# Tracing each convolution of a hybrid SSD/attention block one tile ahead of its user, on one Trainium2 core

## The chip, the cores and the metric

The kernel runs on one core of a Trainium2 chip. The metric is the device time of one execution in microseconds (us). A core has a matrix engine (PE, with its weight loads shown apart as PEld), a vector engine (DVE), a scalar engine for activations (ACT), a general engine (POOL) and a sync engine (SP) whose queue issues most DMAs. Every engine runs its own instructions strictly in the order of its list, and the engines wait for one another through semaphores.

## The reference, cut to what matters

Two layers, each a token mixer followed by a mixture of experts. Layer 0 mixes with a bidirectional Mamba-2 scan (SSD), layer 1 with attention. The change touches the SSD mixer alone:

```python
def project(u):
    z, xbc, dtr = jnp.split(u @ in_w, [D_INNER, D_INNER + CONV_DIM], axis=-1)
    xbc = jax.nn.silu(dwconv_centred(xbc, conv_w, conv_b))          # width 5, per channel
    xs, Bm, Cm = jnp.split(xbc, [...], axis=-1)                     # 2048, 8*128, 8*128 channels
    dt = jax.nn.softplus(dtr... + dt_bias)
def ssd_chunked(xs, dt, A, Bm, Cm, h0):                             # chunks of 128 tokens
    seg = exp(where(tri, acum[..., :, None] - acum[..., None, :], -inf))
    cb = einsum('bclgn,bcsgn->bcgls', Cc, Bc)                       # the product B C, per group
    y_diag = einsum('bcgrls,bcsgrp->bclgrp', cb[:, :, :, None] * seg, xdt)
    states = einsum('bcsgn,bcgrs,bcsgrp->bcgrpn', Bc, decay_end, xdt)
    h = dec * h + st                                                # scan over the chunks
    y_off = einsum('bclgn,bcgrpn,bcgrl->bclgrp', Cc, h_prev, exp(acum))
    return y_diag + y_off
y = y_forward + flip(y_backward) + D_skip * xs
out = rmsnorm(y * silu(z), norm_w) @ out_w
```

There are 1280 tokens (256 context, 1024 latent), that is 10 chunks of 128, 8 groups of B and C with 4 heads of 64 channels each.

## The kernel before, in words

Channels are cut into tiles of 128: 16 tiles of x, 8 of B, 8 of C, 16 of the gate z. **A tile of the convolution** (`conv_tile`) fetches its weights by DMA (L309), splits them into a high part on ACT (L311) and a low part on POOL (L314, twice), and projects the tokens on PE in three blocks of 256, 512 and 512: 72 matmuls at L54 to L56, 24 of them with 256 columns and 48 with 512. ACT copies each block out (L344, L345), DVE adds the other four taps (L349, four times), ACT takes a tangent (L353) and DVE applies it (L354, twice).

**A group** is one tile of B, one of C, the transpose of B (`Btm`), the product B C (`cb`, L513) and then two **cores**, one for each x tile of the group. `core` transposes its x tile (L363), runs the backward states (L396, L382) and then five pairs of chunks. For each pair it needs a decay matrix `Eb`: a DMA on SP's queue spreads a row over the partitions (L405), POOL masks two halves (L408, twice), ACT takes eight exponentials (L413), POOL adds the halves (L416), DVE multiplies by `cb` (L417). There are three `Eb` buffers, so the DMA of pair 4 can start only when pair 1's last output matmul (L463) is done, pair 5's after pair 2's, and the next core's first after pair 3's. The state that enters a chunk goes through PE (L442), DVE (L451) and POOL (`yos`, L452) before PE adds it to the output (L460 with `Eb`, L463 with `yos`). DVE adds the skip term (L467) and SP stores the tile (L469).

**Order.** The lists of the engines are made by a list scheduler: what is traced earlier has priority, and a step takes its place when its inputs and a buffer are free by the scheduler's estimates. A tile's buffers come from pools with a fixed count: one of B (`h_lo`), two each of C, x, raw and of the weights, three PSUM banks for projections (`in_ps`), one for transposes (`tr_ps`, used by L363 and L513), two for outputs (`y_ps`). The gates of the first two z tiles (`gate`, with `halves` giving its two scratch tiles) follow the last core and fill PE beside it; the gates from the third on use other pools.

Of the kernel before, what the change touches and what calls it, by code (L numbers as in the profile page):

```python
# [9 lines left out]
F32 = mybir.dt.float32  # L10
# [8 lines left out]
P = 128  # L19
# [10 lines left out]
NG = 8  # L30
# [10 lines left out]
class Net:  # L41
# [128 lines left out]
    def ssd(self):  # L170
# [53 lines left out]
        gp = tc.alloc_tile_pool(name="grp", bufs=1)  # L224
# [81 lines left out]
        def weights(c0):  # L306

            raw = wp.tile([P, KT, P], F32, name="w_raw")
            nc.sync.dma_start(raw, wv[:, :, c0:c0 + P])  # L309
            w = [wp.tile([P, KT, P], F32R, name=f"w{k}") for k in range(2)]  # L310
            nc.scalar.activation(w[0], raw, AF.Copy)  # L311
            for k in range(0, KT, 4):
                sl = slice(k, k + 4)
                nc.gpsimd.tensor_tensor(w[1][:, sl], raw[:, sl], w[0][:, sl].bitcast(F32), op=OP.subtract)  # L314
            return w

        def proj(w, b, pin=pin):
            t0, n = BLK[b]
            ps = pin.tile([P, 512], F32, name="in_ps")
            for k in range(KT):  # L320
                self.mm3(ps[:, :n], [w[m][:, k] for m in range(2)], [hT(m, k, b) for m in range(2)],
                         k == 0, k == KT - 1)
            return ps[:, :n], t0, n

        PAD = {0: 2, 1: 262, 2: 774}
        PTOK = TOK + 4

        def at(c, n=1):

            o = c * P + (4 if c >= NCT else 0)  # L330
            return slice(o, o + n * P)

        def conv_tile(ci, dst):

            w = weights(DI + ci * P)
            next(mods, None)
            raw = gp.tile([P, 1288], F32, name="raw", bufs=2)
            nc.gpsimd.memset(dst[:, 256:260], 0.0)
            nc.gpsimd.memset(raw[:, 0:2], 0.0)
            nc.gpsimd.memset(raw[:, 258:262], 0.0)  # L340
            nc.gpsimd.memset(raw[:, 1286:1288], 0.0)
            for b in range(3):
                ps, t0, n = proj(w, b)
                nc.scalar.activation(raw[:, PAD[b]:PAD[b] + n], ps, AF.Copy)  # L344
                nc.scalar.activation(dst[:, PAD[b] - 2:PAD[b] - 2 + n], ps, AF.Identity,  # L345
                                     bias=self.pcol[:, 160 + ci:161 + ci], scale=self.pcol[:, 64 + ci:65 + ci])

            for w_ in (0, 1, 3, 4):
                nc.vector.scalar_tensor_tensor(dst, raw[:, w_:w_ + PTOK], self.pcol[:, 32 * w_ + ci:32 * w_ + ci + 1],  # L349
                                               dst, op0=OP.mult, op1=OP.add)  # L350
            for t0, n in ((0, 642), (642, 642)):
                th = raw[:, t0:t0 + n]
                nc.scalar.activation(th, dst[:, t0:t0 + n], AF.Tanh)  # L353
                nc.vector.scalar_tensor_tensor(dst[:, t0:t0 + n], th, 1.0, dst[:, t0:t0 + n], op0=OP.add, op1=OP.mult)  # L354

        def transposed(src, name, pool):

            o = pool.tile([P, NT, P], F32, name=name)
            for c0 in range(0, NT, 4):
                n = min(4, NT - c0)  # L360
                ps = ptp.tile([P, 4, P], F32, name="tr_ps")
                for q in range(n):
                    nc.tensor.transpose(ps[:, q], src[:, at(c0 + q)], self.ident)  # L363
                nc.scalar.activation(o[:, c0:c0 + n], ps[:, :n], AF.Copy)
            return o
# [132 lines left out]
                    nc.scalar.activation(th[:, :n], yd[:, :n], AF.Square)  # L498
                    nc.gpsimd.tensor_tensor(acc[:, t0:t0 + n], first[:, t0:t0 + n], th[:, :n], op=OP.add)

        for g in range(NG):
            BT = hp.tile([P, PTOK], F32, name="BT", tag="h_lo")
            CT = gp.tile([P, PTOK], F32, name="CT", bufs=2)
            conv_tile(16 + g, BT)
            conv_tile(24 + g, CT)
            Btm = transposed(BT, "Btm", gp)
            cb = gp.tile([P, NT, P], F32, name="cb")
            for c0 in range(0, NT, 4):
                n = min(4, NT - c0)
                ps = ptp.tile([P, 4, P], F32, name="tr_ps")  # L510
                for q in range(n):
                    sl = at(c0 + q)
                    nc.tensor.matmul(ps[:, q], BT[:, sl], CT[:, sl], start=True, stop=True)  # L513
                nc.scalar.activation(cb[:, c0:c0 + n], ps[:, :n], AF.Copy)
            for h in range(2):
                xT = gp.tile([P, PTOK], F32, name="xT", bufs=2)
                conv_tile(2 * g + h, xT)
                core(2 * g + h, xT, CT, Btm, cb)
        for _ in mods:
            pass  # L520

# [1 line left out]
        zt = adp.tile([P, 4, 512], F32, name="adw")  # L523
        acc0 = hp.tile([P, TOK], F32, name="acc0", tag="h_lo")
        turns = 0

        def halves():
            nonlocal turns
            turns ^= 2
            return zt[:, turns], zt[:, turns + 1]  # L530
        for ct in range(early):
            gate(ct, weights(ct * P), pin, halves, acc0, acc0 if ct else None)
        for p_ in (pst, ptp, pin, co, gp, adp, cs):
# [983 lines left out]
```

## Time and profile before

| | |
|---|---|
| median of 3 runs | 3840.92 us (3840.58 to 3845.42) |
| the profiled execution's own time | 3852.41 us |
| its span in the trace | 3850.6 us |
| mean granted PE clock over the span | 0.973 |
| PE busy | 3562.8 us, 93% of the span |
| the SSD stage that the change touches | about 130 to 990 us of the span |

Busy time is the time in which an engine worked; what stands in brackets behind an instruction of the trace is the idle time of the engine just before it and what ended it. The granted clock is a share of full speed.

### The profile page before, as it was taken

The numbers are of one execution on the slowest core, as the hardware profiler recorded it, in microseconds if no ns is written. First come the engines' busy times: TensorE is split into PE (matmuls) and PEld (weight loads), VectorE is DVE, ScalarE is ACT, GpSimd is POOL, SyncE is SP. The second block draws the span as 40 slices with busy tenths as digits, with TensorE's granted clock in tenths as the row PEclk, the third lists the DMA queues.
The fourth block names the chain that finished last, engine by engine and source line by source line (L and its number), as shares of the span: only waits on it lengthen the run. The fifth ranks groups of instructions, "written<-read, shape, count | busy, mean of one in ns | idle before, by whom it ended". The sixth has DMA issues, their size and how long they took to land.

```text
span 3850.6 us, 56599 instructions
## 1 busy us (share of the span) xinstructions
PE 3562.8 (93%) x21156; PEld 2674.7 (69%) x21156; DVE 2594.0 (67%) x3675; ACT 2024.8 (53%) x3310; POOL 1811.8 (47%) x1356
## 2 busy tenths in 40 slices
PE   6999999999898998999999998899999976999997
PEld 3776777777787775666666767667777655777765
DVE  4776777777533376666666665555666587999988
ACT  4544444445323234555555545477777534777665
POOL 2345554455443334566666662221111115777786
PEclk8999999999999998999999998999999987999999
DMA  5333422222544336888888872100000346999994
GB/s 191 108 104 116 128 90 83 79 77 90 161 137 142 119 117 244 315 305 311 319 320 304 287 238 91 39 17 1 1 1 12 118 168 265 371 382 379 343 339 163
DMA packets 296803, 681.10 MB, mean 177 GB/s; under 512 B 22568, under 2 KB 148400, under 8 KB 290384
## 3 DMA queue, kind: packets, MB, share of 16 engines
q1 hardware_dynamic: 271824, 615.50, 44.6%
q0 software_dynamic: 12752, 39.33, 4.2%
q10 hardware_dynamic: 11952, 22.65, 1.8%
q8 instruction: 167, 2.74, 0.3%
q14 instruction: 108, 0.88, 0.1%
HBM read 611.97 MB, written 62.82 MB: 175 GB/s over the span
## 4 chain that ended last, share of the span: by engine, by line
PE 37%; DVE 11%; issue 6%; DMA 5%; POOL 4%; ACT 2%; SPq 0%; ACTq 0%; POOLq 0%; DVEq 0%
DVE m_w L728 6%; PE pv L1177 5%; PE S L1143 4%; PE a_tr L1164 4%; PE acc L54 4%; PE acc L56 4%; PE acc L55 4%; POOL m_w L725 3%; PE cacc L695 3%; DMA m_raw<-in_moe_w_dram 3%; PE o_ps L55 1%; PE o_ps L56 1%; PE o_ps L54 1%; PE qkv L56 1%; PE qkv L54 1%
## 5 line engine op out<-in xcount | busy, mean ns | idle before, releaser
L728 DVE TENSOR_TENSOR m_w<-m_raw,m_w 128x1792 fp32r<-128x1792 f32 (+1 forms) x384 | 890.5, 2342 | 251.8 <-ACT m_w L722 249.5
L722 ACT ACTIVATE m_w<-m_raw 128x2048 fp32r<-128x2048 f32 x384 | 732.6, 1916 | 485.9 <-DMA m_raw<-in_moe_w_dram 268.1
L725 POOL TENSOR_TENSOR m_w<-m_raw,m_w 128x256 fp32r<-128x256 f32 (+1 forms) x384 | 824.7, 2175 | 346.1 <-ACT m_w L722 343.5
L54 PE MATMUL in_ps<-hh,w 128*128 128x512 f32 (+1 forms) x1152 | 423.6, 368 | 7.7 <-DVE th L491 7.7
L55 PE MATMUL acc<-m_w,xl 128*128 128x512 f32 x1024 | 407.9, 399 | 22.3 <-DVE m_w L728 13.7
L56 PE MATMUL in_ps<-hh,w 128*128 128x512 f32 (+1 forms) x1152 | 420.7, 365 | 0.0
L55 PE MATMUL in_ps<-hl,w 128*128 128x512 f32 (+1 forms) x1152 | 418.7, 363 | 0.0
L54 PE MATMUL acc<-m_w,xl 128*128 128x512 f32 x1024 | 407.2, 404 | 4.5 <-ACT xl L48 4.5
L56 PE MATMUL acc<-m_w,xl 128*128 128x512 f32 x1024 | 402.1, 393 | 0.0
L413 ACT ACTIVATE Eb<-Eb,ebias 128x128 f32<-128x128 f32 x640 | 199.4, 391 | 165.2 <-POOL Eb L408 163.5
L1147 DVE TENSOR_REDUCE mx<-S 128x1 f32<-128x1024 f32 x128 | 155.7, 1216 | 181.2 <-PE S L1143 179.2
L1194 POOL TENSOR_TENSOR q<-s 64x128 f32<-64x128 f32 x128 | 58.7, 459 | 415.2 <-DVE mx L1152 347.4
L55 PEld LDWEIGHTS acc<-m_w,xl 128*128 128x128 f32 x1024 | 193.9, 189 | 83.9 <-DVE m_w L728 28.8
L54 PEld LDWEIGHTS in_ps<-hh,w 128*128 128x128 f32 x1152 | 220.1, 191 | 45.4 <-issue 10.9
L54 PEld LDWEIGHTS acc<-m_w,xl 128*128 128x128 f32 x1024 | 193.5, 190 | 69.6 <-issue 21.4
L56 PEld LDWEIGHTS in_ps<-hh,w 128*128 128x128 f32 x1152 | 220.0, 191 | 31.1 <-issue 5.0
L55 PEld LDWEIGHTS in_ps<-hl,w 128*128 128x128 f32 x1152 | 219.8, 191 | 29.2 <-issue 3.7
L314 POOL TENSOR_TENSOR w<-w_raw,w 128x512 fp32r<-128x512 f32 x96 | 154.5, 1630 | 166.4 <-ACT w L311 156.0
L56 PEld LDWEIGHTS acc<-m_w,xl 128*128 128x128 f32 x1024 | 193.7, 189 | 38.4 <-DVE xl L49 0.2
L55 PE MATMUL acc<-m_w,gT 128*128 128x512 f32 x512 | 204.4, 399 | 6.6 <-DVE m_w L728 4.1
L54 PE MATMUL acc<-m_w,gT 128*128 128x512 f32 x512 | 202.7, 402 | 1.0 <-ACT gT L48 1.0
L56 PE MATMUL acc<-m_w,gT 128*128 128x512 f32 x512 | 203.1, 397 | 0.0
(390 smaller groups left out, 7658.5 us busy)
## 6 DMA issues: line engine op xcount, KB each, us to landing
m_raw<-in_moe_w_dram SPq DMA_DIRECT2D x384, 1024.0 KB
adw<-in_ada_w_dram SPq DMA_DIRECT2D x48, 1024.0 KB
Eb<-fd SPq DMA_DIRECT2D x80, 512.0 KB
w_raw<-in_ssd_in_w_dram SPq DMA_DIRECT2D x48, 512.0 KB
ydd<-yd SPq DMA_DIRECT2D x80, 128.0 KB
yt_raw<-yzd SPq DMA_DIRECT2D x40, 256.0 KB
xs<-x SPq DMA_DIRECT2D x32, 256.0 KB
h<-h SPq DMA_DIRECT2D x16, 512.0 KB
```

The lines of the kernel that those rows point to most:

```text
L54: mm(out, lhs[0], rhs[0], start=start, stop=False)
L55: mm(out, lhs[0], rhs[1], start=False, stop=False)
L56: mm(out, lhs[1], rhs[0], start=False, stop=stop)
L314: nc.gpsimd.tensor_tensor(w[1][:, sl], raw[:, sl], w[0][:, sl].bitcast(F32), op=OP.subtract)
L413: nc.scalar.activation(Eb[:, d, hh, cc], Eb[:, d, hh, cc], AF.Exp, bias=bias[:, c0 + cc, k:k + 1])
L722: nc.scalar.activation(w[0], raw, AF.Copy)
L725: nc.gpsimd.tensor_tensor(w[1][:, :, n:], raw[:, :, n:], w[0][:, :, n:].bitcast(F32), op=OP.subtract)
L728: nc.vector.tensor_tensor(w[1][:, :, :n], raw[:, :, :n], w[0][:, :, :n].bitcast(F32), op=OP.subtract)
L1143: nc.tensor.matmul(o, qTs[self.qt][:, 2 * self.hp + hh], kT[k][:, self.kv, 512 * b:512 * b + n], start=(k == 0), stop=(k == 1))
L1147: nc.vector.tensor_reduce(self.mx[:, 0:1], S[hh], axis=AX.X, op=OP.max)
L1164: nc.tensor.transpose(ps[:, q], self.pr[hh][:, (c0 + q) * P:(c0 + q + 1) * P], net.ident)
L1177: nc.tensor.matmul(self.pv[o:o + 64, 0], v32[:, t, self.kv], self.PT[:, t], start=(t < 2), stop=(t >= NT - 2))
```

## The change

Two helpers trace a pair B, C (`tile_BC`) and a tile of x (`tile_x`). B and C of group 0 are traced ahead of the loop. In group g the order is now: x tile 2g, transpose of B and product B C, x tile 2g+1, core 2g, B and C of group g+1, core 2g+1. The line of the product B C is L524 afterwards, L513 before. In the early gates, the y tile goes through four buffers in turn instead of two, and the tangent is kept in a tile of the convolution's `raw` buffers. No instruction of arithmetic is added or taken away.

```diff
@@ -498,11 +498,22 @@
                     nc.scalar.activation(th[:, :n], yd[:, :n], AF.Square)
                     nc.gpsimd.tensor_tensor(acc[:, t0:t0 + n], first[:, t0:t0 + n], th[:, :n], op=OP.add)
 
-        for g in range(NG):
+        def tile_BC(g):
             BT = hp.tile([P, PTOK], F32, name="BT", tag="h_lo")
             CT = gp.tile([P, PTOK], F32, name="CT", bufs=2)
             conv_tile(16 + g, BT)
             conv_tile(24 + g, CT)
+            return BT, CT
+
+        def tile_x(ct):
+            xT = gp.tile([P, PTOK], F32, name="xT", bufs=2)
+            conv_tile(ct, xT)
+            return xT
+
+        BC = tile_BC(0)
+        for g in range(NG):
+            BT, CT = BC
+            xT = [tile_x(2 * g)]
             Btm = transposed(BT, "Btm", gp)
             cb = gp.tile([P, NT, P], F32, name="cb")
             for c0 in range(0, NT, 4):
@@ -512,10 +523,11 @@
                     sl = at(c0 + q)
                     nc.tensor.matmul(ps[:, q], BT[:, sl], CT[:, sl], start=True, stop=True)
                 nc.scalar.activation(cb[:, c0:c0 + n], ps[:, :n], AF.Copy)
-            for h in range(2):
-                xT = gp.tile([P, PTOK], F32, name="xT", bufs=2)
-                conv_tile(2 * g + h, xT)
-                core(2 * g + h, xT, CT, Btm, cb)
+            xT.append(tile_x(2 * g + 1))
+            core(2 * g, xT[0], CT, Btm, cb)
+            if g + 1 < NG:
+                BC = tile_BC(g + 1)
+            core(2 * g + 1, xT[1], CT, Btm, cb)
         for _ in mods:
             pass
 
@@ -526,8 +538,8 @@
 
         def halves():
             nonlocal turns
-            turns ^= 2
-            return zt[:, turns], zt[:, turns + 1]
+            turns = (turns + 1) % 4
+            return zt[:, turns], gp.tile([P, 1288], F32, name="raw", bufs=2)[:, :512]
         for ct in range(early):
             gate(ct, weights(ct * P), pin, halves, acc0, acc0 if ct else None)
         for p_ in (pst, ptp, pin, co, gp, adp, cs):
```

How the lists move, counted in PE's list (steady state, groups 4 to 6):

| between | before | after |
|---|---|---|
| last projection matmul of an even x tile and the first transpose (L363) of its core | 56 projection matmuls | 72 |
| the same, odd x tile | 59 | 144 |
| last projection matmul of C and the first product B C | 52 | 115 |
| last output matmul (L463) of pair 1 and first (L460) of pair 4, even core | 14 of 512 columns, 27 small | 6 of 512, 21 of 256, 26 small |
| the same, odd core | 14 of 512, 27 small | 5 of 512, 24 of 256, 29 small |
| last output matmul of pair 2 and first of pair 5, even core | 15 of 512, 22 small | 16 of 512, 20 of 256, 23 small |
| the same, odd core | 15 of 512, 22 small | 10 of 512, 24 of 256, 29 small |

Small are the matmuls of 128 columns at L363, L396, L429, L442, L460, L463, L513.

On DVE, where the convolution of an even x tile (`xT_6131`) ends and its core begins, in the list before:

```order
L417 TENSOR_TENSOR Eb_6286<-Eb_6286,cb_6114 128x512
L417 TENSOR_TENSOR Eb_6314<-Eb_6314,cb_6114 128x512
L417 TENSOR_TENSOR Eb_6349<-Eb_6349,cb_6114 128x512
L349 SCALAR_TENSOR_TENSOR xT_6131<-raw_6139,pcol_64,xT_6131 128x1284 x4
L354 SCALAR_TENSOR_TENSOR xT_6131<-raw_6139,xT_6131 128x642 x2
L370 TENSOR_TENSOR xw1_6251<-xtm_6233,wst_137 128x256
L370 TENSOR_TENSOR xw0_6304<-xtm_6233,wst_137 128x256
L370 TENSOR_TENSOR xw0_6332<-xtm_6233,wst_137 128x256
L378 COPY H1_6250<-st_ps_6253 128x128
```

In the list after, the first instruction of a core's scan (`xw1_6838`, whose transposed x came from the tile `xT_6233`) has this around it:

```order
L417 TENSOR_TENSOR Eb_6901<-Eb_6901,cb_6216 128x512
L349 SCALAR_TENSOR_TENSOR CT_6617<-raw_6726,pcol_64,CT_6617 128x1284
L370 TENSOR_TENSOR xw1_6838<-xtm_6820,wst_137 128x256
L349 SCALAR_TENSOR_TENSOR CT_6617<-raw_6726,pcol_64,CT_6617 128x1284
L378 COPY H1_6837<-st_ps_6840 128x128
L349 SCALAR_TENSOR_TENSOR CT_6617<-raw_6726,pcol_64,CT_6617 128x1284
L382 SCALAR_TENSOR_TENSOR H1_6837<-H1_6837,dec_138,st_ps_6840 128x64
L349 SCALAR_TENSOR_TENSOR CT_6617<-raw_6726,pcol_64,CT_6617 128x1284
L382 SCALAR_TENSOR_TENSOR H1_6837<-H1_6837,dec_138,st_ps_6840 128x64
L370 TENSOR_TENSOR xw1_6846<-xtm_6820,wst_137 128x512
```

Before, the core's first L370 stands directly behind the two L354 that finish its own x tile; after, it stands between the taps of the next group's C tile, and its own x tile ended 39 rows earlier.

On POOL, around pair 2 of an odd core, where `w1` is the low part of the weights of a later tile and `yos` the entering state of a pair, before:

```order
L314 TENSOR_TENSOR w1_8143<-w_raw_8140,w0_8142 128x512 x2
L452 TENSOR_TENSOR yos_7766<-yos_7766 128x2x128
L408 AFFINE_SELECT Eb_7783<-Eb_7783 128x512 x2
L452 TENSOR_TENSOR yos_7813<-yos_7813 128x2x128
L452 TENSOR_TENSOR yos_7856<-yos_7856 128x2x128
L416 TENSOR_TENSOR Eb_7783<-Eb_7783 128x512
```

The same place of the list after (core 13):

```order
L314 TENSOR_TENSOR w1_8910<-w_raw_8907,w0_8909 128x512 x2
L452 TENSOR_TENSOR yos_7970<-yos_7970 128x2x128
L452 TENSOR_TENSOR yos_8017<-yos_8017 128x2x128
L408 AFFINE_SELECT Eb_7987<-Eb_7987 128x512 x2
L452 TENSOR_TENSOR yos_8060<-yos_8060 128x2x128
L408 AFFINE_SELECT Eb_8034<-Eb_8034 128x512 x2
L416 TENSOR_TENSOR Eb_7987<-Eb_7987 128x512
L408 AFFINE_SELECT Eb_8396<-Eb_8396 128x512 x2
```

In both lists the weight split stands ahead of pair 2's `yos`, and one more pair of masks has moved up before the last `yos`. What the split waits for has moved: it needs the weight buffer of two tiles earlier, and the last matmul on that buffer stands 16 rows of PE's list ahead of pair 2's first L463 here, where it stood 73 rows ahead before (21 and 64 rows in the even cores).

On PE, at the end of the last core (15), pair 4 and the gate of the second z tile (`w_9009`, `w_9010`) before:

```order
L56 MATMUL in_ps<-hh,w_9010 128x512
L54 MATMUL in_ps<-hh,w_9009 128x512
L55 MATMUL in_ps<-hl,w_9009 128x512
L56 MATMUL in_ps<-hh,w_9010 128x512
L460 MATMUL y_ps<-Eb,xtm 64x128 x2
L463 MATMUL y_ps<-ident,yos 128x128
L460 MATMUL y_ps<-Eb,xtm 64x128 x2
L463 MATMUL y_ps<-ident,yos 128x128
L54 MATMUL in_ps<-hh,w_9009 128x512
L55 MATMUL in_ps<-hl,w_9009 128x512
```

And pairs 4 and 5 there in the list after (`w_9012`, `w_9013` are the second z tile's weights, `w_9159` the third's):

```order
L442 MATMUL yo_ps<-H_8641,CT 128x128
L442 MATMUL yo_ps<-H_8856,CT 128x128
L442 MATMUL yo_ps<-H_8641,CT 128x128
L460 MATMUL y_ps<-Eb,xtm 64x128 x2
L463 MATMUL y_ps<-ident,yos 128x128
L460 MATMUL y_ps<-Eb,xtm 64x128 x2
L463 MATMUL y_ps<-ident,yos 128x128
L460 MATMUL y_ps<-Eb,xtm 64x128 x2
L463 MATMUL y_ps<-ident,yos 128x128
L460 MATMUL y_ps<-Eb,xtm 64x128 x2
L463 MATMUL y_ps<-ident,yos 128x128
L54 MATMUL in_ps<-hh,w_9159 128x256
```

Before, gate matmuls stand on both sides of pair 4's outputs; after, the second z tile is used up, and pairs 4 and 5 stand directly behind the L442 with no projection matmul between them.

From the gate of the fourth z tile on, the lists of all engines are the same before and after.

## Rows read from the trace of the kernel before

**Rows 1.** Page, busy time by engine, whole span.

```profile
PE 3562.8 (93%) x21156; PEld 2674.7 (69%) x21156; DVE 2594.0 (67%) x3675; ACT 2024.8 (53%) x3310; POOL 1811.8 (47%) x1356
```

**Rows 2.** Stretches: busy us (count) of PE, PEld, DVE, ACT, POOL; clock; DMA share; GB/s.

```profile
130.00:990.00 860.00, 799.54 (x4856) 626.58 (x4854) 614.49 (x1139) 414.40 (x1033) 422.70 (x483) 0.99 0.32 100
...
738.00:743.00 5.00, 4.35 (x21) 3.42 (x22) 3.44 (x7) 2.36 (x8) 1.73 (x7) 0.70 0.35 118
```

**Rows 3.** Waits of PE, 90 to 1080 us: total us, times, longest us.

```profile
PE y_ps L460 <- DVE Eb L417: 18.2, 24, 3.2
PE y_ps L460 <- issue: 16.9, 13, 1.7
PE tr_ps L513 <- DVE CT L354: 9.7, 7, 1.6
PE tr_ps L363 <- DVE xT L354: 8.4, 8, 1.3
PE in_ps L54 <- DVE th L491: 7.7, 2, 4.0
```

**Rows 4.** Timeline of PE, an even core in mid-stage: start, length, instruction, idle before.

```profile
704.82 0.63 PE L363 MATMUL tr_ps<-ident,xT 128*128 128x128 f32 x4 [0.99 <-DVE xT L354]
...
722.27 0.49 PE L463 MATMUL y_ps<-ident,yos 128*128 128x128 f32 x2
...
726.55 0.49 PE L463 MATMUL y_ps<-ident,yos 128*128 128x128 f32 x2
...
734.00 0.44 PE L460 MATMUL y_ps<-Eb,xtm 128*64 128x128 f32 x4 [0.51 <-DVE Eb L417]
...
736.41 0.39 PE L54 MATMUL in_ps<-hh,w 128*128 128x512 f32 x1
736.63 0.39 PE L55 MATMUL in_ps<-hl,w 128*128 128x512 f32 x1
738.65 0.44 PE L460 MATMUL y_ps<-Eb,xtm 128*64 128x128 f32 x4 [1.63 <-issue]
```

**Rows 5.** Timeline of SP's queue, the same core.

```profile
722.38 0.37 SPq L405 DMA_DIRECT2D Eb<-fd  x1
```

**Rows 6.** Timeline of POOL, the same core.

```profile
713.47 2.53 POOL L314 TENSOR_TENSOR w<-w_raw,w 128x512 fp32r<-128x512 f32 x2 [7.83 <-ACT w L311]
723.21 0.73 POOL L452 TENSOR_TENSOR yos<-yos 128x256 f32<-128x256 f32 x1 [7.21 <-DVE yos L451]
726.05 1.23 POOL L408 TENSOR_SCALAR_AFFINE_SELECT Eb<-Eb 128x512 f32<-128x512 f32 x2 [2.11 <-DMA Eb<-fd]
...
730.27 1.28 POOL L416 TENSOR_TENSOR Eb<-Eb 128x512 f32<-128x512 f32 x1
```

**Rows 7.** Timeline of ACT, the same core.

```profile
712.33 1.06 ACT L311 ACTIVATE w<-w_raw 128x1024 fp32r<-128x1024 f32 x1 [3.87 <-PE in_ps L55]
...
726.72 2.45 ACT L413 ACTIVATE Eb<-Eb,ebias 128x128 f32<-128x128 f32 x8 [9.57 <-POOL Eb L408]
```

**Rows 8.** Timeline of DVE, the same core.

```profile
730.93 1.97 DVE L349 SCALAR_TENSOR_TENSOR xT<-raw,pcol,xT 128x1284 f32<-128x1284 f32 x1
732.83 1.12 DVE L417 TENSOR_TENSOR Eb<-Eb,cb 128x512 f32<-128x512 f32 x1
...
737.36 1.20 DVE L417 TENSOR_TENSOR Eb<-Eb,cb 128x512 f32<-128x512 f32 x1 [2.41 <-POOL Eb L416]
```

**Rows 9.** Durations by line (ns, least/median/greatest), 130 to 990 us.

```profile
L408 POOL TENSOR_SCALAR_AFFINE_SELECT Eb<-Eb x160: 632/640/1904, 153.8 to 981.0; 128x512 f32<-128x512 f32 x160
L349 DVE SCALAR_TENSOR_TENSOR xT<-raw,pcol,xT x64: 1540/1556/2633, 138.8 to 943.5; 128x1284 f32<-128x1284 f32 x64
L314 POOL TENSOR_TENSOR w<-w_raw,w x62: 1272/1297/2628, 136.9 to 964.2; 128x512 fp32r<-128x512 f32 x62
```

**Rows 10.** Timeline of PE at the end of core 15: pairs 4 and 5.

```profile
984.88 0.44 PE L460 MATMUL y_ps<-Eb,xtm 128*64 128x128 f32 x4 [3.22 <-DVE Eb L417]
...
988.67 0.67 PE L460 MATMUL y_ps<-Eb,xtm 128*64 128x128 f32 x4
```

## The prediction

> **What bounds the kernel now.** I read the busy table first: PE works 93% of the span [rows 1], so the kernel is PE-bound and time comes only from PE's gaps. The change lies in the SSD stage. In the table of stretches PE works 799.5 of the 860 us there [rows 2]: 60 us of gaps. The list of PE's waits then says what ends them [rows 3]. Four groups matter. PE waits 9.7 us for C's last vector step before the product B C (7 times) and 8.4 us for x's last vector step before a core's transposes (8 times): together 18.1 us. It waits 35.1 us (18.2 + 16.9) before an output matmul L460 that needs a decay matrix; the second row says "issue", but in the timeline that wait ends at 738.65 [rows 4], and the multiply by `cb` on DVE ran from 737.36 for 1.20 us [rows 8], so it is the same wait and I count both as one. The last, 7.7 us before L54, is in the gates from the fourth on, whose lists don't change.
>
> The timeline of one core shows the second kind. After pair 1's outputs (722.27) PE has work until 733.49 and then idles 0.51 us before pair 4; before pair 5 it idles 1.63 us [rows 4]. The chain that it waits for starts with pair 1, whose `Eb` buffer pair 4 takes: DMA issue at 722.38 [rows 5], masks from 726.05 [rows 6], exponentials from 726.72 for 2.45 us [rows 7], add from 730.27 for 1.28 us [rows 6], multiply from 732.83 for 1.12 us [rows 8], output at 734.00. That is 11.7 us from 722.27, of which 1.1 us is queueing on POOL ahead of the add (729.17 to 730.27) and 1.3 us queueing behind a tap L349 on DVE (731.55 to 732.83). Without both it is 9.3 us.
>
> After such a gap the granted clock is low: 0.70 in 738 to 743 us, against 0.99 over the stage [rows 2]. One per cent of 799.5 us is 8 us lost by that.
>
> **The change part by part.** The sum is made against the profiled execution's own 3852.4 us, which is 11.5 us over the median of the runs; I carry that difference unchanged.
>
> *Waits for the convolution.* In the list after, 72 or 144 projection matmuls stand between an x tile and its core's transposes, 56 or 59 before; and 115 instead of 52 between C and the product. Matmuls of 512 columns follow each other at 0.22 to 0.23 us (736.41, 736.63) [rows 4], so 16 more are 3.7 us at most and, of 256 columns, half that by columns (an estimate): 1.8 us, over a wait of 0.99 [rows 4], at longest 1.3 us [rows 3]. The 63 more ahead of the product outdo its 1.6 us. Both waits go: -18.1 us. What is late next behind them is the scan itself: its first vector instruction now stands among the taps of another tile, 1.56 us each [rows 9], but PE has that tile's matmuls to do, so I price it at nothing; uncovered it would be one tap per core, 16 x 1.56 = 25 us.
>
> *Waits before the outputs.* A small matmul row costs (11.22 - 14 x 0.23) / 27 = 0.30 us by the stretch from 722.27 to 733.49 (counts in the table of the change). After, PE's work from pair 1 to pair 4 is, even core, 6 x 0.23 + 21 x 0.115 + 26 x 0.30 = 11.6 us; odd core, 5 x 0.23 + 24 x 0.115 + 29 x 0.30 = 12.6 us; 11.2 before. From pair 2 to pair 5 it is 12.9 and 13.8 us, against 15 x 0.23 + 22 x 0.30 = 10.1 before, where the chain took 738.65 - 726.55 = 12.1 us [rows 4]. So the usual chain (11.7, 12.1) is nearly always covered. It grows when a mask or an add meets a tap: masks reach 1.90 us for a usual 0.64, taps 2.63 for 1.56 [rows 9], so 1.3 + 1.1 = 2.4 us more, which makes 14.1 and would leave 2.5 us in an even core and 1.5 in an odd one. Bounds over the stage: 0 to 35. Half of those collisions give 1.2 and 0.7 us, in 8 and 7 cores 15 us: -20 us.
>
> Here a rule of the Trainium skill bears on it: "SBUF — State Buffer", section "Who interferes with whom", says that a vector instruction with two SBUF inputs and a GpSimd instruction that reads SBUF exclude each other, and the first to start blocks the other. The trace agrees in kind: the taps and the masks have just those long cases [rows 9]. It speaks against the change, which moves taps into the tail of cores where masks and adds run; what it would do when every core meets it is the second rival.
>
> *Clock.* Fewer gaps, half the loss back: -4 us (bounds 0 and -8).
>
> *Entering state of pair 2.* The weight split on POOL now waits for matmuls that stand only 16 rows (odd core) or 21 rows (even core) ahead of the first L463 of pair 2, 73 and 64 before. Behind it on POOL stands that pair's `yos`. The split chain is 1.06 (L311) [rows 7], 2.53 (L314 twice) and 0.73 (L452) [rows 6]: 4.3 us without hand-overs. PE's rows cover 15 or 16 x 0.30 = 4.6 us in odd cores and 17 x 0.30 + 4 x 0.115 = 5.6 in even ones. Before, POOL idled 7.21 us between the two [rows 6], so it cost nothing. With both splits at their longest, 2.63 us [rows 9], the chain is 7.1 us: at most 2.5 us in odd, 1.5 in even cores. Bounds 0 and 8 x 2.5 + 8 x 1.5 = 32 us; the typical durations stand next to the cover, so I take 0.3 us per core: +5 us. It also delays pair 2's and so pair 5's chain by as much as PE, which cancels.
>
> *ACT behind the next tile.* The copies of the product B C now stand behind evacuations L345 whose x buffer comes free with the last L467 of the odd core. No row shows such a wait; bounds per group are nothing, since three PSUM banks hold that tile meanwhile, and a wait as long as that before a core's transposes, 0.99 us [rows 4], so 0 to 8 us over the stage; nearer to nothing, +2 us.
>
> *End of core 15.* The second gate is used up, so pair 4 has 3 x 0.23 + 26 x 0.30 = 8.5 us of cover for 11.7: a wait of 3.2 us, as the 3.22 us there now [rows 10]; pair 5 has only 2 matmuls more and 22 rows, and waits 2 us more where it followed within 4 us before [rows 10]; the clock after it costs another 2 us. +4 us (bounds 0 and 8).
>
> *Early gates.* Four y buffers and other scratch tiles add no instruction. They let loads start earlier; the gates' matmuls do not wait there now [rows 3], so 0, between -1 and +2.
>
> Sum: -18.1 - 20 - 4 + 5 + 2 + 4 = -31 us. 3852.4 - 31 = 3821.4; less 11.5 is **3810 us**. Behind the stage the lists are the same, so nothing gives it back.
>
> **Rivals.**
> *All stage waits go.* Every chain stays under its cover, the split chain too: -18.1 - 35 - 8 + 4 = -57, 3784 us. For it: 11.6 to 13.8 us of cover for 11.7 and 12.1. Against: the even core's margin is nil at pair 4, and the table of durations has long cases [rows 9].
>
> *The taps meet the masks in every core.* The chain is 14.1 us each time, 8 x 2.5 + 7 x 1.5 = 31 of the 35 us stay: -18.1 - 4 + 5 + 2 + 4 = -11 with no clock regained, 3830 us; with the delayed product added, up to 3838. For it: DVE's two-input steps and POOL's masks fill most of the stage, DVE 614 and POOL 423 of 860 us [rows 2]. Against: the medians of masks, taps and splits lie within 0.03 us of their least [rows 9], so long cases are the few. This is the result that the rule above gives.
>
> *Slower: the split chain becomes the bound.* Weight split and `yos` in series behind the last matmul of the tile, 7.1 us each time, 32 us, while the waits before the outputs stay at 31 of 35 because every later chain starts that much later and the three buffers are still three: -18.1 - 4 + 32 + 2 + 4 = +16, and 4 more of clock for the added gaps: +20, 3861 us. It decides from (18.1 + 4 - 6) / 16 = 1.0 us per core on, if the outputs' waits stay, or (18.1 + 20 + 4 - 6) / 16 = 2.3 us per core if they fall as I forecast. For it: POOL's order puts the split directly ahead of `yos`. Against: the chain is 4.3 us by typical durations.
>
> *The change does not do what it says.* The convolution's waits only move: PE's list has its gap at the scan's first vector step, 0.5 to 1.5 us per core, 8 to 24 us, in place of 18.1; outputs as in the second rival. 3834 to 3850, about no change.
>
> **How the numbers follow.** Forecast 0.52, with its own range 3796 to 3823; all waits gone 0.13; taps and masks 0.16; slower 0.10; no effect 0.09. Between them the range 3784 to 3840 leaves out half of the first rival, the slower one and half of the last. A difference of 0.2% (7.7 us, 3833 to 3849 being the same) is about what a measurement of this kernel can tell from no change. Faster: 0.52 + 0.13 + two thirds of 0.16 + a little of the last, 0.77. Same: the rest of those, 0.12. Slower: 0.11.
>
> **What would show it.** In the waits of PE after: the two rows behind L354 are gone or under 2 us together; the rows before L460 fall from 35.1 us to 10 to 20; a row for L463 behind POOL's `yos` appears with about 5 us; the stretch of the stage has PE busy a few per cent denser at a clock not under 0.99; core 15 shows pair 4 and pair 5 both waiting, 5 us together. Wrong if the waits before L460 stay at 30 us or more, if L463 waits over 1.5 us per core, or if waits appear before L396 or L429 behind L370, the scan's vector steps among another tile's taps.

## The result: slower by 0.6%, and the profile after

The changed kernel takes 3865.3 us (3862.43 to 3868.27, 4 runs) against 3840.75 beside it: a ratio of 1.006, 95% interval 1.0048 to 1.0073, 24.6 us slower where 31 us less were forecast. Its profiled execution took 3862.43 us. The two profiles differ by less, because that of before was 11.5 us over its median; so I compare the stage. Both lists are the same behind the early gates, and the last gate's tangent step on DVE (L491) is the common end mark: 1201.2 us before, 1221.3 after. A second execution of before's cores, with only the gates changed (first experiment), has it at 1195.6. The stage lost 20 to 26 us, which is the whole difference.

The stretches to those marks, of after, of before, and of that second execution (columns as in [rows 2]):

```profile
90.00:1222.00 1132.00, 1055.84 (x6099) 847.24 (x6098) 732.00 (x1299) 500.31 (x1180) 514.01 (x563) 0.97 0.34 105
```

```profile
90.00:1202.00 1112.00, 1041.69 (x6089) 831.91 (x6088) 734.27 (x1295) 501.12 (x1180) 522.90 (x563) 0.99 0.35 106
```

```profile
90.00:1196.00 1106.00, 1033.95 (x6081) 825.48 (x6079) 737.79 (x1291) 500.02 (x1180) 523.71 (x563) 1.00 0.34 106
```

PE idles 76.2 us after (1132.00 less 1055.84), 70.3 and 72.0 before: only 4 to 6 us more. The rest of the loss is in PE's busy time, and the third column from the right says why: the granted clock is 0.97 where it was 0.99 and 1.00. Adding up the stretches at the half level (1.2 GHz) in the clock record between those marks gives 78.5 us after, 27.3 and 10.2 before. In such a stretch a matmul of 512 columns takes 0.43 us for 0.23, so that up to half of it is lost. Pairs of executions of one order give the price. The second and the third line (one order up to the early gates) differ by 17.1 us of half clock and by 7.7 us of PE's busy time, and the pair e10, e11 below by 20.5 and 8.4, that is 0.41 to 0.45 us for each us at half clock. By that price (an estimate) the clock costs 21 to 31 us more after than before. PE's busy time rose by 14 to 22 us only, so 6 to 9 us of it were saved elsewhere; that gain isn't attributed.

PE's waits after, from 90 to 1090 us, answer to [rows 3]:

```profile
PE y_ps L460 <- DVE Eb L417: 43.9, 17, 4.0
PE st_ps L396 <- DVE xw L370: 11.6, 19, 1.6
...
PE yo_ps L442 <- DVE H L378: 4.0, 5, 0.8
PE tr_ps L363 <- ACT xtm L364: 3.7, 5, 1.9
...
PE y_ps L460 <- issue: 1.3, 3, 0.6
...
PE y_ps L463 <- POOL yos L452: 0.6, 1, 0.6
PE y_ps L460 <- DVE yd L467: 0.3, 1, 0.3
```

The two groups behind L354 are gone. In their place stand three at the start of the scan: L396 behind the first weighting of x (L370), L442 behind the first state, the transposes behind ACT, 11.6 + 4.0 + 3.7 = 19.3 us. Ahead of the outputs PE waits 45.5 us (43.9 + 1.3 + 0.3). In the kernel before it was 35.1 us, or 37.6 with two small rows that [rows 3] doesn't have:

```profile
PE y_ps L460 <- ACT Eb L413: 1.8, 1, 1.8
...
PE y_ps L460 <- PE tr_ps L363: 0.7, 2, 0.5
```

In 12 of the 16 cores it is now one wait of 2.6 to 4.0 us ahead of pair 4, and 2.2 in core 15, where a core in mid-stage had two of 0.5 and 1.6 [rows 4]; cores 0, 2 and 4 wait 0.2 us or less before it.

An even core in mid-stage, PE's timeline as in [rows 4]:

```profile
633.72 0.49 PE L463 MATMUL y_ps<-ident,yos 128*128 128x128 f32 x2
...
643.93 0.39 PE L56 MATMUL in_ps<-hh,w 128*128 128x512 f32 x1
647.29 0.44 PE L460 MATMUL y_ps<-Eb,xtm 128*64 128x128 f32 x4 [2.97 <-DVE Eb L417]
...
649.97 0.63 PE L55 MATMUL in_ps<-hl,w 128*128 128x512 f32 x1
650.40 0.63 PE L56 MATMUL in_ps<-hh,w 128*128 128x512 f32 x1
```

Pair 1 ends at 633.72, PE runs out of work at 644.32 (647.29 less 2.97), and after the wait the matmuls of 512 columns follow at 0.43 us (649.97 to 650.40) where they follow at 0.23 at full clock. The granted clock there and behind the next core's wait of 3.48 us (700.39):

```profile
648.00:652.00 4.00, 4.00 (x16) 2.96 (x16) 4.00 (x5) 1.17 (x4) 4.00 (x3) 0.60 0.47 162
700.00:704.00 4.00, 3.61 (x16) 2.54 (x17) 2.19 (x3) 1.45 (x5) 4.00 (x3) 0.50 0.16 54
```

The chain to pair 4 in that core, on SP's queue, POOL, ACT and DVE, as in [rows 5] to [rows 8]:

```profile
634.15 0.38 SPq L309 DMA_DIRECT2D w_raw<-in_ssd_in_w_dram  x1
634.64 0.67 SPq L405 DMA_DIRECT2D Eb<-fd  x1
```

```profile
639.84 1.23 POOL L408 TENSOR_SCALAR_AFFINE_SELECT Eb<-Eb 128x512 f32<-128x512 f32 x2 [2.86 <-DMA Eb<-fd]
641.92 2.25 POOL L408 TENSOR_SCALAR_AFFINE_SELECT Eb<-Eb 128x512 f32<-128x512 f32 x2 [0.86 <-DMA Eb<-fd]
644.16 0.71 POOL L452 TENSOR_TENSOR yos<-yos 128x256 f32<-128x256 f32 x1
644.84 1.25 POOL L416 TENSOR_TENSOR Eb<-Eb 128x512 f32<-128x512 f32 x1
```

```profile
640.51 2.46 ACT L413 ACTIVATE Eb<-Eb,ebias 128x128 f32<-128x128 f32 x8 [7.79 <-POOL Eb L408]
```

```profile
630.40 0.42 DVE L370 TENSOR_TENSOR xw<-xtm,wst 128x256 f32<-128x256 f32 x1
...
641.53 1.55 DVE L349 SCALAR_TENSOR_TENSOR BT<-raw,pcol,BT 128x1284 f32<-128x1284 f32 x1
646.12 1.11 DVE L417 TENSOR_TENSOR Eb<-Eb,cb 128x512 f32<-128x512 f32 x1 [3.04 <-POOL Eb L416]
```

A weight load L309 stands 0.5 us ahead of pair 4's decay load, and the first mask starts 5.2 us behind the issue of that (634.64 to 639.84), where it was 3.7 [rows 5, 6]. The masks of pair 5, beside a tap (641.53), take 2.25 us instead of 1.23, and with a `yos` they stand ahead of pair 4's add: exponentials are done at 642.97, the add starts at 644.84. So the chain took 13.6 us (633.72 to 647.29) instead of 11.7, and PE had 10.6 us of work (633.72 to 644.32).

The weight load stands there, 0.5 or 1.1 us ahead, in cores 6 to 13 alone. From the decay load's issue to the first mask it is 5.0 to 5.8 us in these and 3.8 to 4.1 us in the other eight. Cores 1, 3 and 5 have none within 16 us and wait 3.13 us all the same. Core 5, on POOL, ACT and PE:

```profile
472.70 1.23 POOL L408 TENSOR_SCALAR_AFFINE_SELECT Eb<-Eb 128x512 f32<-128x512 f32 x2 [0.62 <-DMA Eb<-fd]
476.74 1.27 POOL L314 TENSOR_TENSOR w<-w_raw,w 128x512 fp32r<-128x512 f32 x1 [2.81 <-PE in_ps L56]
...
479.86 1.25 POOL L416 TENSOR_TENSOR Eb<-Eb 128x512 f32<-128x512 f32 x1
```

```profile
473.37 2.44 ACT L413 ACTIVATE Eb<-Eb,ebias 128x128 f32<-128x128 f32 x8 [2.39 <-POOL Eb L408]
```

```profile
482.94 0.44 PE L460 MATMUL y_ps<-Eb,xtm 128*64 128x128 f32 x4 [3.13 <-DVE Eb L417]
```

Pair 4's exponentials are done at 475.81, but on POOL a weight split stands ahead of the add and waits 2.81 us for a projection matmul of PE (L56), as the prediction said of it; behind it come a `yos` and the masks of another pair. So the add starts 4.05 us behind them (479.86). Cores 2 and 4, which have neither a weight load nor a split in the way, don't wait. So what stands ahead of pair 4's chain isn't the same in all cores: on SP's queue a weight load, or on POOL's list a split or another pair's masks.

At the start of the next even core, on DVE and POOL:

```profile
720.92 1.56 DVE L349 SCALAR_TENSOR_TENSOR xT<-raw,pcol,xT 128x1284 f32<-128x1284 f32 x1 [1.43 <-ACT xT L345]
722.39 1.50 DVE L370 TENSOR_TENSOR xw<-xtm,wst 128x256 f32<-128x256 f32 x1
```

```profile
719.81 3.80 POOL L314 TENSOR_TENSOR w<-w_raw,w 128x512 fp32r<-128x512 f32 x2 [1.04 <-ACT w L311]
```

The first weighting L370 waits behind a tap, and then itself takes 1.50 us instead of 0.42 (630.40, above), while the weight split of POOL (3.80 us instead of the 2.53 of [rows 6]) runs beside it. In 12 more cores it takes 1.48 to 1.51 us behind a tap, beside a split or an add on POOL. That agrees with the rule of the Trainium skill that the prediction cites ("SBUF — State Buffer", section "Who interferes with whom"), at a place that the prediction had not considered.

### The profile page after: what moved, and what is told of

Read it like the earlier page. It is cut to its first block, busy times and chain, and to the rows that moved or that the text cites. A ratio compares the mean times of both kernels' runs of the same rounds, so it can differ in the third digit from the quotient of the medians.

```text
span 3860.2 us, 56557 instructions
## 1 busy us (share of the span) xinstructions
PE 3578.3 (93%) x21156; PEld 2693.9 (70%) x21156; DVE 2590.8 (67%) x3675; ACT 2023.7 (52%) x3310; POOL 1798.6 (47%) x1356
## 4 chain that ended last, share of the span: by engine, by line
PE 38%; DVE 11%; issue 6%; POOL 4%; DMA 4%; ACT 2%; SPq 0%; POOLq 0%; ACTq 0%; DVEq 0%
DVE m_w L740 6%; PE pv L1189 5%; PE S L1155 4%; PE a_tr L1176 4%; PE acc L54 4%; PE acc L56 4%; PE acc L55 4%; PE cacc L707 4%; POOL m_w L737 3%; DMA m_raw<-in_moe_w_dram 2%; PE o_ps L55 1%; PE o_ps L54 1%; PE o_ps L56 1%; PE qkv L56 1%; PE qkv L54 1%
## 5 line engine op out<-in xcount | busy, mean ns | idle before, releaser
L56 PE MATMUL in_ps<-hh,w 128*128 128x512 f32 (+1 forms) x1152 | 423.8, 368 | 0.0
L56 PE MATMUL acc<-m_w,xl 128*128 128x512 f32 x1024 | 401.9, 393 | 0.0
L55 PEld LDWEIGHTS acc<-m_w,xl 128*128 128x128 f32 x1024 | 193.3, 189 | 81.7 <-DVE m_w L740 27.3
L56 PEld LDWEIGHTS in_ps<-hh,w 128*128 128x128 f32 x1152 | 223.0, 194 | 32.2 <-issue 4.2
L56 PEld LDWEIGHTS acc<-m_w,xl 128*128 128x128 f32 x1024 | 193.7, 189 | 38.5 <-DVE xl L49 0.2
L56 PE MATMUL acc<-m_w,gT 128*128 128x512 f32 x512 | 202.8, 397 | 0.1
```

The costliest lines, as they stand in the source:

```text
L55: mm(out, lhs[0], rhs[1], start=False, stop=False)
L56: mm(out, lhs[1], rhs[0], start=False, stop=stop)
```

## The experiments

Ratios are to the kernel before on the same chip, with 95% intervals; the changed kernel has 1.006.

**Only the gates, and only the tiles.** `e1_gates_only` is before with the change in `halves()`, `e2_tiles_only` is after without it.

```diff
-            turns ^= 2
-            return zt[:, turns], zt[:, turns + 1]
+            turns = (turns + 1) % 4
+            return zt[:, turns], gp.tile([P, 1288], F32, name="raw", bufs=2)[:, :512]
```

> The kernel before with only the change to the early gates (y in four buffers, tangent in a raw tile). Theory A (the loss comes from the cores: one long wait before pair 4's outputs in every core, and a lower granted clock behind it): 3836 to 3846 us, no difference from before. Theory B (the loss comes from the early gates, whose matmuls and scratch tiles now meet the last cores): 3855 us or more.

> The changed kernel with the early gates as before. Theory A: 3858 to 3872 us, as the changed kernel; PE waits of 40 to 45 us before L460. Theory B: 3835 to 3848 us.

1.000 (0.999 to 1.0009), 3837.06 us; and 1.0065 (1.0046 to 1.0085), 3863.81 us, with 41.8 us of waits before L460 behind DVE. The early gates count for nothing; the loss is the convolution's order.

**One kind of tile at a time.**

```diff
 e5_x_only:
-        BC = tile_BC(0)
-            BT, CT = BC
+            BT, CT = tile_BC(g)
-            if g + 1 < NG:
-                BC = tile_BC(g + 1)
 e6_BC_only:
-            xT = [tile_x(2 * g)]
-            xT.append(tile_x(2 * g + 1))
-            core(2 * g, xT[0], CT, Btm, cb)
+            core(2 * g, tile_x(2 * g), CT, Btm, cb)
+            xT = tile_x(2 * g + 1)
...
```

> The changed kernel with only the two x tiles of a group traced ahead, B and C at the start of their group as before. Theory A (which part shifts the weight load in front of the decay load?): if the x tiles do it, the long wait before pair 4 stays in each core, 3855 to 3875 us; if B and C do it, 3830 to 3845 us. The waits before the product B C (9.7 us) are back in both.

> The changed kernel with only B and C of the next group traced ahead of the second core, each x tile directly ahead of its core as before. Theory A: the waits before the product B C go (-9.7 us), those before the transposes stay (8 us); if the long wait before pair 4 comes with the B and C tiles it shows in the odd cores alone, 8 x 3 us and the clock behind them, 3845 to 3860 us; if it comes with the x tiles, 3828 to 3838 us.

x alone: 1.0082 (1.0064 to 1.0101). B and C alone: 1.0033 (1.0022 to 1.0045). That is 3867.7 and 3848.99 us. Both are slower, x more. Each expectation had one branch by which the other kind of tile does it, 3845 us at most for x alone and 3838 for B and C alone, and both of these missed: neither part is free. Their waits differ from those of the changed kernel. With x alone:

```profile
PE y_ps L460 <- DVE Eb L417: 27.3, 18, 3.6
PE y_ps L463 <- POOL yos L452: 12.8, 13, 2.2
PE st_ps L396 <- DVE xw L370: 11.9, 14, 1.3
PE tr_ps L523 <- ACT cb L524: 10.6, 4, 2.7
```

Here the entering state is late (12.8 us before L463), which the forecast had priced at 5; in the changed kernel it is 0.6.

**The weight load behind the decay loads.** `e7_load_behind` is after with this edit (cut; `last_eb` keeps the last decay load of each core):

```diff
-            nc.sync.dma_start(raw, wv[:, :, c0:c0 + P])
+            with tc.issue_after(behind.ins) if behind else nullcontext():
+                nc.sync.dma_start(raw, wv[:, :, c0:c0 + P])
...
-            conv_tile(16 + g, BT)
+            conv_tile(16 + g, BT, last_eb.get(2 * g - 4))
-            conv_tile(ct, xT)
+            conv_tile(ct, xT, last_eb.get(ct - 3) if ct % 2 == 0 else None)
```

> The changed kernel, but the weight load that its trace shows directly ahead of pair 4's decay load on SP's queue is issued behind pair 5's decay load of that core. Theory A (the weight load delays the decay load by 1.5 to 2 us, 5.2 and 5.7 us from issue to the first mask instead of 3.7): the wait before pair 4 falls from about 3.1 to 1.5 us a core, PE's waits before L460 from 45 to 20 or 25 us, and with the clock 3830 to 3848 us. Rival C (the shorter stretch of PE work between pair 1 and pair 4 and POOL's order decide): waits stay at 38 us or more, 3856 to 3868 us.

1.0015 (1.0005 to 1.0024), 3840.53 us: about 18 of the 24.6 us come back. But the waits before L460 behind DVE stay at 41.0 us. An even core on PE (its lines stand three later):

```profile
620.89 0.49 PE L466 MATMUL y_ps<-ident,yos 128*128 128x128 f32 x2
...
632.49 0.44 PE L463 MATMUL y_ps<-Eb,xtm 128*64 128x128 f32 x4 [2.70 <-DVE Eb L420]
```

The chain is 11.6 us (620.89 to 632.49), 2 us shorter, as expected; the scheduler, which placed the lists anew, also left only 8.9 us of work in it (to 629.79). So each core ends earlier and still waits: both theories are half right. That the chain is shorter without the load is shown; that the 18 us come by it is not, since the order changed with it. In cores 0 to 11 no weight load stands within 16 us ahead of pair 4's decay load any more, and ten of these twelve still wait 1.4 to 3.6 us: the load alone doesn't make the wait. Idle time (76.3 us) and half clock (71.7 us) up to its end mark of 1206.9 us are nearly those of after; the time came out of the small matmuls (all but those of the projections): from the start of one to the start of the next, with steps above 0.75 us left out, it adds up to 298 us, 309 in after. Why is open. `e12_before_load` was to be the control, the same edit in before.

> The kernel before with two of a group's four weight loads (B and the first x tile) queued behind the last decay load of a core, as e7_load_behind does in the changed kernel. There a weight load stood 6 us ahead of pair 4's decay load. Theory A (the gain of 18 us in e7 came from taking the weight load out of the way of the decay load, which only the changed order put there): 3830 to 3845 us, no difference from before. Rival G (the loads cost something wherever they stand, and moving them helps any order): 3825 us or less.

1.0206 (1.0186 to 1.0226): neither. Two loads a group now stood behind the cores' last decay loads, weights came late (PE waited 9.1 us for POOL's split) and the states came late too (13.0 us before L432, the states' matmul there, behind DVE). It says nothing on e7 and stays a failed control.

**Four buffers for the half of the decay matrix that the output uses.**

```diff
-                Eb = co.tile([P, 2, 2, 2, P], F32, name="Eb", bufs=3)
-                nc.sync.dma_start(Eb.rearrange(...), rows(fd, [0, P], [TOK, 4], ...))
+                Eb = [co.tile([P, 2, 2, P], F32, name=f"Eb{d}", bufs=(4, 2)[d]) for d in range(2)]
+                for d in range(2):
+                    nc.sync.dma_start(Eb[d].rearrange(...), rows(fd, [0, P], [TOK, 2], ...))
...
```

> The changed kernel with the decay matrix in two tiles: the half that the output uses has four buffers instead of three, the other half, which is dead after the add, has two; the same space, twice as many loads of half the size. Pair 4's load no longer waits for pair 1's outputs, pair 5's waits for pair 1's. Theory A (the chain through the three buffers makes the long wait): waits before L460 under 10 us, clock back at 0.985 or more, 3805 to 3830 us. Rival P (DVE and POOL have too little time in a core, so that the wait only moves to another place): 3845 us or more, waits before L463 or L460 of 30 us or more.

> The kernel before with the same two tiles for the decay matrix. Theory A: the 35 us of waits before L460 fall under 10 us and the clock rises a little: 3798 to 3818 us, faster than both kernels, and the convolution's waits (18 us) stay. Rival P: 3830 us or more.

After: 1.0191 (1.0174 to 1.0208). Before: 1.0117 (1.0098 to 1.0135). These are 3904.32 and 3879.25 us, in the ranges of rival P. Theory A fell: the waits behind the decay matrix fall to a few us, and others take their place. PE's waits in e3, and ACT at one of them:

```profile
PE y_ps L464 <- POOL yos L453: 30.8, 19, 5.6
PE tr_ps L363 <- ACT xtm L364: 26.4, 16, 3.2
PE tr_ps L525 <- ACT cb L526: 13.7, 5, 3.1
```

```profile
695.91 0.99 ACT L414 ACTIVATE Eb<-Eb,ebias 128x128 f32<-128x128 f32 x3 [3.04 <-POOL Eb L409]
696.80 0.57 ACT L364 ACTIVATE xtm<-tr_ps 128x512 f32<-128x512 f32 x1
```

The copy of the transposed x (L364, 696.80) stands on ACT behind exponentials that waited 3.04 us for POOL's masks. That reads as if the scheduler, with one more buffer, puts decay work ahead of the scan's own steps, so that the three buffers had kept decay work back as well as late. It is argued from this place and not shown: the same edit also doubles the number of loads and leaves the other half two buffers instead of three, and no run separates the three.

**Filling the long wait with matmuls.** e8 is after, e9 is e7, with

```diff
+                for _ in range(6 if c0 == 6 else 0):
+                    nc.tensor.matmul(y.rearrange("p c l -> p (c l)"), xtm[:, c0], spare[c0], start=True, stop=True,
+                                     skip_group_check=True)
```

where `spare` is the second half of pair 4's `Eb`.

> The changed kernel with six matmuls of 256 columns, whose results are overwritten, ahead of pair 4's outputs in every core: 16 x 6 x 0.43 = 41 us of matrix work added, 2.6 us a core, ready when pair 4's exponentials are, so that they fall into the wait of 3 us. The order shows that they push some 1.5 us of projection matmuls from before pair 4 to behind it. Theory K (most of the loss is the half clock behind each long gap, 78 us of half clock between 90 and 1222 us, 27 before): half clock under 40 us, that is 20 us or more back, against 16 x 1.5 = 24 us pushed back: 3853 to 3872 us, no slower than the changed kernel. Theory W (the loss is the waiting itself, and the clock counts little): the chain sets the end of each core as before and the pushed matmuls come on top: 3880 to 3900 us.

> The kernel with the weight loads behind the decay loads (e7_load_behind), and the same six matmuls ahead of pair 4's outputs in every core. Theory K: the gaps of 2.7 to 3.6 us that e7 keeps are filled, half clock falls from 72 to under 40 us: 3830 to 3848 us, no slower than e7's 3840. Theory W: 3860 us or more.

e8: 1.009 (1.0065 to 1.0115), 3873.48 us, 8 us over after by the times and 12 by the ratios; half clock 47.8 us where 78.5 were. So 41 us of matrix work cost 8 to 12. By theory K's prices it is 24 - 15 = +9; by theory W +24. That is nearer to K, though just outside both of the ranges. e9: 1.0121 (1.0092 to 1.015), 3884.66 us, 44 us over e7 (41 by the ratios), half clock still 64.9: in that order the wait moved to pair 5 (2.5 us), and theory K's forecast failed there. So one of two agrees with theory K, and these runs don't isolate the clock's price.

**The start of the cores ahead of the next tile.** e10 is after, e11 is e7, with `core` cut in two:

```diff
+            h0 = head(2 * g, xT[0], Btm)
             xT.append(tile_x(2 * g + 1))
-            core(2 * g, xT[0], CT, Btm, cb)
+            core(2 * g, xT[0], CT, Btm, cb, *h0)
+            h1 = head(2 * g + 1, xT[1], Btm)
             if g + 1 < NG:
```

> The changed kernel with the start of each core (transposes of x and the backward states) traced ahead of the next convolution tile, so that its vector steps have priority over the taps of that tile. Theory A (the 19 us of waits at the scan's start, 11.6 before L396, 4.0 before L442, 3.7 before the transposes, are what replaced the convolution's 18 us): they fall under 6 us, the wait before the transposes for the x tile may come back with up to 8 us, the long wait before pair 4 stays: 3846 to 3860 us. Rival D (the scan's start is covered anyway and the core's end is set by the decay chain): 3860 us or more.

> The same start of the cores, and the weight loads behind the decay loads as in e7_load_behind (3840.5 us). Theory A: the two gains add, 3820 to 3835 us, at or below the kernel before. Rival D: 3838 us or more.

e10: 1.0037 (1.0026 to 1.0048), 3853.08 us, in the range of theory A. Its waits:

```profile
PE tr_ps L363 <- DVE xT L354: 20.2, 7, 3.5
PE y_ps L464 <- issue: 14.4, 15, 2.6
...
PE y_ps L464 <- DVE Eb L421: 6.1, 5, 2.0
PE st_ps L396 <- DVE xw L370: 6.0, 8, 1.9
```

The scan's start waits 6.0 us instead of 11.6, but the wait for x is back, longer than before (20.2 us in 7 waits, 3.5 at the longest, against 8.4 us in 8); that before the outputs fell to 20.5, which the theory had not said; half clock is 51.2 us. e11: 1.0048 (1.0031 to 1.0065), 3854.24 us, outside theory A's range. But it doesn't test whether the gains add: in e10 no weight load stands within 5 us ahead of pair 4's decay load, and the traces of e10 and e11 show the same order on every engine up to the end mark, and on SP's queue. So they are two executions of one order. Up to the end mark both idle 67.3 us; half clock is 51.2 and 30.7 us, and PE's busy time 1054.9 and 1046.5. That is the clock's price used above: 8.4 us for 20.5.

None of the versions of the changed order beat the kernel before; e7 came nearest.

## Why the prediction was wrong, by its steps

- *Waits for the convolution*, -18.1 us: right in itself, both rows are gone. "What is late next behind them is the scan itself" was named and priced at nothing, with 25 us if uncovered. It measured 19.3 us. The cover was counted in matmuls of the next tile, but the weighting step is first in PE's path to L396, and it met both a tap and POOL's work. e10, which gives the start priority, took 9 to 12 us off the total, though other waits moved with it.
- *Waits before the outputs*, -20 us: **the step that failed**; the clock, below, fell with it. +8 to +10 us was measured. The cover was 10.6 us for a forecast 11.6, as a small matmul row took (10.6 - 1.4 - 2.4) / 26 = 0.26 us for the 0.30 that I drew from before; and the chain was 13.6 us for 11.7, not a rare case: it took 13.5 to 14.4 us in the twelve cores that wait. In the core shown, from pair 1's end to the first mask it was 6.1 us (633.72 to 639.84) for 3.8, that is 2.3 more, behind the weight load; POOL's queue ahead of the add grew by 0.8, from 1.1 to 1.9; and the tap that stood ahead of the multiply before (1.3) no longer does. In cores 1, 3 and 5 it was POOL's queue ahead of the add alone, 4.05 us for 1.1 in core 5. "Half of those collisions" was a guess without a row.
- *Entering state of pair 2*, +5 us: I saw that the weight split moves to pair 2, and followed POOL's queue. At the `yos` nothing was lost (0.6 us). But the split's wait for PE came as forecast, 2.81 us in core 5, and in cores 1, 3 and 5 pair 4's add stood behind it; I had followed POOL's queue to `yos` only. And in cores 6 to 13 the next weight load went on SP's queue ahead of pair 4's decay load; I had not followed the DMA of the moved tile past that queue.
- *Clock*, -4 us: by the clock record +21 to +31 (an estimate, by the price above), the largest term. The prediction set out from "time comes only from PE's gaps"; here PE's gaps grew by 4 to 6 us and its busy time by 14 to 22. The sum of idle time hardly rose, but in most cores it is gathered in one gap of some 3 us, and at 12 of the 13 waits of 2.2 us or more before pair 4 the clock goes to half, for 3.4 to 10.2 us. Before, up to 1000 us, it did so behind three gaps of 1.6 to 1.7 us and the one of 3.2. That the gathering is what costs the clock is argued from this and from e8; no run changes the gaps alone.
- *ACT behind the next tile*, +2, and *end of core 15*, +4: 0.2 us, and 2.2 + 0.6 us at pairs 4 and 5 for 3.2 before. *Early gates*, 0: right, as e1 shows.

Of the rivals, the one that taps meet masks names the right place, but held 31 us of waits for 45 measured and no loss of clock; that its chain of 14.1 us is near the 13.5 to 14.4 measured is luck in part, since a weight load and POOL's order make it. The slower one had the right sign, 3861 us for 3865, mostly by luck: PE hardly waits for `yos`, and the split delays pair 4's add in three cores, not in all. The last rival had the scan's start right, 8 to 24 us for 19.3. Two of the prediction's own signs of being wrong came: the waits before L460 stayed over 30 us, and L396 waits behind L370. The 6 to 9 us by which PE's busy time is shorter apart from the clock, and e7's gain, stay open.

## What to carry to other kernels

Tracing a producer earlier also moves what it frees: follow each buffer to the transfer or the step that waits for it, and see what that stands ahead of on its queue or list. Count a wait not only by its sum but by its longest gap: here nearly the same idle time (70.3 and 76.2 us), gathered in longer pieces, went with three times the half clock (27.3 and 78.5 us). A scheduler places its lists anew with each edit, so that one cause taken away (a load, a buffer) can come back as another wait. And before an edit is read as an experiment, compare its order with that of its base: e11's was that of e10.

## What was not expected of the hardware

Seventy-eight of 1132 us at half clock for a PE that was 93% busy; that one order, run twice, can differ by 20.5 us of half clock and 8.4 us of time (e10 and e11); and that 41 us of added matmuls cost only 8 to 12, while a fourth decay buffer in the same space, with twice as many loads, cost 1.2% over before and 1.3% over after.
